# The last 32 dense tokens of a PEER layer: activations from gathered rows instead of a chunked product

## The chip, the cores and the metric

The kernel runs on one core of a Trainium2 chip. The metric is the device time of one launch in microseconds, as the median over several runs. A profile is one further execution, recorded by the hardware profiler. TensorE (PE) multiplies matrices and PEld is its weight load; VectorE (DVE), ScalarE (ACT) and GpSimd (POOL) work elementwise; SyncE (SP) only issues DMAs.

## What is computed

One decoder block over 512 tokens of width 1024. The change touches its second half, a PEER layer over 128 x 128 = 16384 experts of one neuron each:

```python
q = (xb @ w_pq).reshape(-1, PEER_HEADS, PEER_QDIM)          # 8 heads
s1 = einsum('thd,hkd->thk', q1, sub_k1); s2 = einsum('thd,hkd->thk', q2, sub_k2)
v1, i1 = top_k(s1, 16); v2, i2 = top_k(s2, 16)
cand = v1[..., :, None] + v2[..., None, :]
sc, ci = top_k(cand, 16)                                    # 16 experts per head, 128 per token
e = i1[ci // 16] * 128 + i2[ci % 16]
g = softmax(sc)
act = gelu(einsum('thkd,td->thk', peer_u[e], xb))
out = einsum('thk,thkd->td', g * act, peer_v[e])
```

Each token chooses 128 experts, takes the dot product of its row h2 with their rows of `peer_u`, applies GELU, weighs with g, and sums rows of `peer_v`. A LayerNorm follows.

## The kernel before

The 512 tokens are four tiles of 128 (P). The tiles 0 to 2 (DENSE = 3, SD = 384 tokens) are computed densely: all 16384 experts in NCH = 128 chunks of 128, first `act = gelu(U_chunk^T h2)` with the tokens as the 384 moving columns of a matmul, then the product of `act` with a dense weight matrix G (zero where a token has not chosen the expert), and last `acc += (act * G)^T V_chunk` into six PSUM banks of 128 x 512. Tile 3 is computed sparsely: 128 gathers of rows of `peer_u` and 128 of `peer_v`, each 128 rows of 4 KB, by indirect DMAs on GpSimd's queue, each multiplied on VectorE.

All products of float32 are made from three (`mm3`): each operand is split into a high part (ScalarE, `load_split2`, L450) and a low part, hi x hi + hi x lo + lo x hi. A chunk of U is 8 x 3 = 24 matmuls of 384 columns (L62 to L64), a chunk of V 3 x 2 x 3 = 18 of 512 columns (`V_products`, L797 to L801). The low part is made on GpSimd (L456) while `last["pool"]` is set, that is until the end of the top-k, and on VectorE (L458) from then on.

The stages of the second half, in the order of the program:

- 16 `query` and `scores` steps. After each, `pump(QPUMP)` runs background work of VectorE: `rows_h2` (h2 of tile 3 by rows, h2n), then one generator `topk_head(h)` per head.
- The main loop runs chunks of U as long as background work is left: the rest of the heads, `topk_last` (tile 3), `softmax`, then `spread`. Chunks until the end of the top-k are "spilled": `act` goes to DRAM (Ad) and comes back later.
- `spread` builds G: for 24 groups of TG = 16 tokens (q = 0 to 7 of each tile t) it makes one-hot matrices of the two index halves on VectorE (L631 to L635, f16), multiplies them on TensorE (L643, L644), scales on ScalarE into `stg` (L645) and writes G to DRAM (Gd). The first NRES = 21 chunks of this stage stay in SBUF ("resident", `U_resident`): their `act` and G are multiplied in place (L651, L653, L705). Further chunks, and VDLY = 3 more, are spilled.
- V of the 21 resident chunks, with GR = 1.8 steps of the gather of tile 3 per chunk.
- The rest in pairs: U and V of one chunk, with GUV = 2.9 gather steps per pair. G is loaded in runs of 8 chunks (1536 KB), and `wf = act * G` is made on VectorE (L778).
- V of the spilled chunks: `ar` brings four chunks of `act` back by one DMA (768 KB), G as before; the gather steps that are left are shared among all but the last six chunks. 260 steps stand for the whole gather.

Pacing is by credits. A generator yields the microseconds that its author declares for what it just issued, and `pump` spends a sum of them after each chunk of U:

```python
    def pump(us):
        credit[0] += us
        while credit[0] > 0 and bg:
            try:
                credit[0] -= next(bg[0])
            except StopIteration:
                bg.pop(0)
```

Before, the sum is 5.5 per query step (QPUMP), 1.1 + 1.2 = 2.3 per chunk until the end of the top-k (UPUMP), 5 in the spread (GPUMP). The order of instructions on an engine is in the end the framework's: it places an instruction by its own reckoning of when operands and buffers are ready, so that work can run ahead of its place in the program. So `rows_x1` (L495), issued in the stage of pairs, executes at 490 us, as soon as xhat is there, in the buffer `facc1`. `behind(a, b)` puts instruction a behind b in its queue. The row buffers of all gathers are four (tag "rows").

## Time and profile before

| | |
|---|---|
| median of 3 runs | 1719.38 us (1719.3 to 1720.42) |
| the profiled execution | 1727.59 us |
| its span, first to last instruction | 1725.9 us |
| mean granted TensorE clock | 0.991 of full |
| TensorE busy | 1668.0 us (97%) |
| VectorE busy | 1353.8 us (78%) |
| DMA | 409.92 MB, mean 238 GB/s |

The span is cut into stages by what runs: queries from about 485 us, chunks of U beside the top-k to 724, the spread to 885, the resident chunks' V to about 985, pairs to 1545, V of the spilled chunks to 1717, then the last LayerNorms. In the rows below a line of code stands as L and its number; PE and PEld are TensorE's matmuls and weight loads. A matmul's record lasts longer than the distance to the next, because matmuls overlap: the distance between starts is what counts.

### The profile page before, as it was taken

How to read it: one execution, taken by the hardware profiler on the slowest of the kernel's cores; microseconds unless marked ns; L12 is line 12 of the kernel's file. 1: busy time of each engine (PE TensorE's matmuls, PEld its weight loads, DVE VectorE, ACT ScalarE, POOL GpSimd, SP SyncE). 2: the span in 40 equal slices, each digit the busy share in tenths (PEclk: the TensorE clock that was granted, in tenths of full speed). 3: DMA queues.
4: the chain of work that ended last, by engine and by line, in shares of the span. 5: the costliest groups of instructions: out<-in, count | busy, mean ns of one | idle time of the engine just before them, and what ended most of it. 6: DMA issues, size and time to landing. Idle time of an engine off the chain costs nothing.

```text
span 1725.9 us, 23559 instructions
## 1 busy us (share of the span) xinstructions
PE 1668.0 (97%) x8658; PEld 1442.8 (84%) x8658; DVE 1353.8 (78%) x2509; ACT 685.9 (40%) x1095; POOL 481.5 (28%) x334
## 2 busy tenths in 40 slices
PE   6999999999999999899999999999999999989997
PEld 3765777788788999899998789999999999978886
DVE  6467786454589999999978888778787888878787
ACT  3467632233343333355543233333333333333333
POOL 2000000000043455400014444444454545531202
PEclk9999999999999999999999999999999999999999
DMA  7602257642252355556699999999899999899982
GB/s 269 201 1 74 98 196 245 219 146 86 77 189 78 103 173 172 191 206 224 211 321 365 363 325 340 320 338 351 312 337 324 326 345 324 311 351 316 305 282 86
DMA packets 162071, 409.92 MB, mean 238 GB/s; under 512 B 22337, under 2 KB 69473, under 8 KB 161698
## 3 DMA queue, kind: packets, MB, share of 16 engines
q1 hardware_dynamic: 112178, 245.35, 42.3%
q0 software_dynamic: 36960, 134.50, 21.6%
q10 hardware_dynamic: 12816, 28.55, 4.3%
q8 instruction: 68, 1.11, 0.3%
q14 instruction: 49, 0.40, 0.1%
HBM read 377.07 MB, written 31.01 MB: 236 GB/s over the span
## 4 chain that ended last, share of the span: by engine, by line
PE 55%; DVE 18%; DMA 5%; issue 4%; POOL 2%; ACT 0%; SPq 0%; DVEq 0%; POOLq 0%; ACTq 0%
PE acc L801 8%; PE acc L800 8%; PE acc L797 8%; PE psU L64 7%; PE psU L62 6%; PE psU L63 6%; DMA wa<-in_w_ada_dram 2%; POOL ru L667 2%; DMA ru<-in_peer_u_dram,idx 1%; DMA rawV<-in_peer_v_dram 1%; PE pso L63 1%; PE pso L64 1%; PE psga L64 1%; PE psga L62 1%; PE pspa L64 1%
## 5 line engine op out<-in xcount | busy, mean ns | idle before, releaser
L64 PE MATMUL psU<-h2Thi,loU 128*128 128x384 f32 x1008 | 340.6, 338 | 5.4 <-DVE loU L458 5.3
L62 PE MATMUL psU<-h2Thi,hiU 128*128 128x384 f32 x1008 | 340.8, 338 | 0.0
L63 PE MATMUL psU<-h2Tlo,hiU 128*128 128x384 f32 x1008 | 339.3, 337 | 0.0
L797 PE MATMUL acc<-hiV,wh 128*128 128x512 f32 x768 | 300.1, 391 | 4.5 <-ACT wh L782 4.5
L800 PE MATMUL acc<-loV,wh 128*128 128x512 f32 x768 | 301.5, 393 | 1.5 <-DVE loV L458 1.5
L801 PE MATMUL acc<-hiV,wl 128*128 128x512 f32 x768 | 301.1, 392 | 0.3 <-DVE wl L783 0.3
L667 POOL DMA_INDIRECT ru<-in_peer_u_dram,idx x128 | 159.0, 1242 | 360.6 <-DVE ru L671 341.2
L680 POOL DMA_INDIRECT rv<-in_peer_v_dram,idx x128 | 176.4, 1378 | 247.9 <-DVE facc L686 226.6
L458 DVE TENSOR_TENSOR loV<-rawV,hiV 128x1024 fp32r<-128x1024 f32 x128 | 156.4, 1222 | 101.2 <-ACT hiV L450 100.9
L450 ACT ACTIVATE hiV<-rawV 128x1024 fp32r<-128x1024 f32 x128 | 135.1, 1055 | 224.2 <-PE psU L63 184.1
L450 ACT ACTIVATE hiU<-rawU 128x1024 fp32r<-128x1024 f32 x126 | 134.0, 1063 | 194.5 <-PE psU L63 105.5
L64 PEld LDWEIGHTS psU<-h2Thi,loU 128*128 128x128 f32 x1008 | 190.4, 189 | 7.7 <-DVE loU L458 7.6
L63 PEld LDWEIGHTS psU<-h2Tlo,hiU 128*128 128x128 f32 x1008 | 190.6, 189 | 2.6
L62 PEld LDWEIGHTS psU<-h2Thi,hiU 128*128 128x128 f32 x1008 | 190.4, 189 | 2.6
L797 PEld LDWEIGHTS acc<-hiV,wh 128*128 128x128 f32 x768 | 144.9, 189 | 33.7 <-ACT wh L782 5.1
L671 DVE SCALAR_TENSOR_TENSOR ru<-ru,h2n 128x1024 f32<-128x1024 f32 x128 | 154.4, 1221 | 22.0 <-DMA ru<-in_peer_u_dram,idx 21.8
L800 PEld LDWEIGHTS acc<-loV,wh 128*128 128x128 f32 x768 | 144.8, 189 | 32.0 <-DVE loV L458 3.1
L801 PEld LDWEIGHTS acc<-hiV,wl 128*128 128x128 f32 x768 | 144.8, 189 | 31.1 <-DVE wl L783 0.7
L686 DVE SCALAR_TENSOR_TENSOR facc<-rv,wg,facc 128x1024 f32<-128x1024 f32 x126 | 159.4, 1278 | 11.7 <-DMA rv<-in_peer_v_dram,idx 11.7
L456 POOL TENSOR_TENSOR lopq<-rawpq,hipq 128x1024 fp32r<-128x1024 f32 x16 | 40.7, 2544 | 325.1 <-ACT hipq L450 325.1
L782 ACT ACTIVATE wh<-wf 128x384 fp32r<-128x384 f32 x107 | 56.2, 526 | 183.4 <-DVE wf L778 100.5
L458 DVE TENSOR_TENSOR loU<-rawU,hiU 128x1024 fp32r<-128x1024 f32 x95 | 115.7, 1218 | 1.4 <-ACT hiU L450 1.4
(628 smaller groups left out, 2942.4 us busy)
## 6 DMA issues: line engine op xcount, KB each, us to landing
rawU<-in_uT_dram SPq DMA_DIRECT2D x128, 512.0 KB
rawV<-in_peer_v_dram SPq DMA_DIRECT2D x128, 512.0 KB
wa<-in_w_ada_dram SPq DMA_DIRECT2D x48, 512.0 KB
G<-Gd SPq DMA_DIRECT2D x11, 1536.0 KB
Gd<-stg ACTq DMA_DIRECT2D x24, 592.0 KB
rawpq<-in_w_pq_dram SPq DMA_DIRECT2D x16, 512.0 KB
Ad<-act ACTq DMA_DIRECT2D x38, 192.0 KB
ar<-Ad SPq DMA_DIRECT2D x9, 768.0 KB
```

The source lines that it names most:

```text
L62: nc.tensor.matmul(ps, l.hi, r.hi, start=(i == 0), stop=False)
L63: nc.tensor.matmul(ps, l.hi, r.lo, start=False, stop=False)
L64: last = nc.tensor.matmul(ps, l.lo, r.hi, start=False, stop=(i == n - 1))
L450: h = nc.scalar.activation(hi, raw, AF.Copy)
L458: last["dve"] = nc.vector.tensor_sub(lo, raw, hi.bitcast(F32))
L667: d = nc.gpsimd.indirect_dma_start(out=rows, out_offset=None, in_=I["peer_u"], in_offset=bass.IndirectOffsetOnAxis(ap=idx[:, s:s + 1], axi ...
L671: paced(nc.vector.scalar_tensor_tensor(rows, rows, 1.0, h2n, op0=ALU.mult, op1=ALU.mult, accum_out=wg[:, s:s + 1]))
L680: nc.gpsimd.indirect_dma_start(out=rows, out_offset=None, in_=I["peer_v"], in_offset=bass.IndirectOffsetOnAxis(ap=idx[:, s:s + 1], axis=0))
L686: paced(nc.vector.scalar_tensor_tensor(fa, rows, wg[:, s:s + 1], fa, op0=ALU.mult, op1=ALU.add))
L797: m = nc.tensor.matmul(acc, l.hi, r.hi, start=st, stop=False)
L800: nc.tensor.matmul(acc, l.hi, r.lo, start=False, stop=False)
L801: nc.tensor.matmul(acc, l.lo, r.hi, start=False, stop=sp_)
```

## The change

The dense tokens become SU = 352 plus GX = 32. Chunks of U have 352 moving columns. For the last 32 tokens of tile 2 the activations of just the 128 chosen experts each are computed: `gather_x` copies the 32 x 128 indices into 128 partitions x 32 columns, gathers 32 times 128 rows of `peer_u`, multiplies each with h2x (the rows h2 of those 32 tokens, four times below each other) and sums, then applies GELU. The activations go into the weights before the one-hots are multiplied (`weights_x`, scaled by the largest value per token, and the scale put back on `stg`), and `act` of those columns is 1 everywhere. The steps of `gather_x` are spread over `topk_last` (one after every second step) and `spread` (one per group until none is left). The credits change: 2.0 per chunk for the heads (HPUMP), 2.8 from `topk_last` on (UPUMP, now without the 1.2), 4.0 in the spread (GPUMP).

```diff
@@ -26,16 +26,20 @@
 DENSE = 3
 SD = DENSE * P
 TG = 16
+GX = 32
+SU = SD - GX
+X0 = P - GX
 
 NTAIL = 4
 FPOOL = {0: 2, 1: 2, 2: 0, DENSE: 0}
-UPUMP = 1.1
+HPUMP = 2.0
+UPUMP = 2.8
 GUV = 2.9
 GU = 0
 NPRE = 2
 PLO = 1
 QPUMP = 5.5
-GPUMP = 5
+GPUMP = 4.0
 VDLY = 3
 NRES = 21
 GR = 1.8
@@ -389,10 +393,11 @@
 
         def early_U(i):
             w = load_split(I["uT"][i], f"U{i}")
-            ps = pmm.tile([P, D], F32, name=f"psU{i}", tag="ss", bufs=1)[:, 0:SD]
-            mm3(ps, [(w[:, k, :], h2T[:, k, 0:SD]) for k in range(NK)])
+            ps = pmm.tile([P, D], F32, name=f"psU{i}", tag="ss", bufs=1)[:, 0:SU]
+            mm3(ps, [(w[:, k, :], h2T[:, k, 0:SU]) for k in range(NK)])
             a = gp.tile([P, S], F32, name=f"act{i}", tag="mt", bufs=2)[:, 0:SD]
-            nc.scalar.activation(a, ps, AF.Gelu)
+            nc.scalar.activation(a[:, 0:SU], ps, AF.Gelu)
+            nc.gpsimd.memset(a[:, SU:SD], 1.0)
             nc.sync.dma_start(Ad[i], a)
 
         for hh in range(2):
@@ -432,6 +437,10 @@
     actp = ctx.enter_context(tc.tile_pool(name="actp", bufs=1, reuse_waits="tile"))
     gat = ctx.enter_context(tc.tile_pool(name="gat", bufs=1, reuse_waits="tile"))
     pu = ctx.enter_context(tc.tile_pool(name="pu", bufs=1, space=PS, reuse_waits="tile"))
+
+    acts = [actp.tile([P, SD], F32, name=f"act{i}") for i in range(4)]
+    for a in acts:
+        nc.gpsimd.memset(a[:, SU:SD], 1.0)
     last = {}
 
     def behind(ins, other):
@@ -465,6 +474,7 @@
 
 
     bg = []
+    last["upump"] = HPUMP
 
     credit = [0.0]
 
@@ -478,14 +488,45 @@
 
 
     h2n = gat.tile([P, D], F32, name="h2n", tag="facc0", bufs=1)
+    h2x = gat.tile([P, D], F32, name="h2x", tag="facc1", bufs=1)
 
     def rows_h2():
         g2r, b2r = (gat.tile([P, D], F32, name=nm, tag="rows", bufs=4) for nm in ("g2r", "b2r"))
         nc.sync.dma_start(g2r, rowsD[2].partition_broadcast(P))
         nc.sync.dma_start(b2r, rowsD[3].partition_broadcast(P))
-        nc.vector.tensor_mul(h2n, xhat[:, DENSE, :], g2r)
-        nc.vector.tensor_add(h2n, h2n, b2r)
-        yield 2.4
+        for t, h in ((DENSE - 1, h2x), (DENSE, h2n)):
+            nc.vector.tensor_mul(h, xhat[:, t, :], g2r)
+            nc.vector.tensor_add(h, h, b2r)
+            yield 2.4
+        for p in range(0, X0, GX):
+            nc.gpsimd.dma_start(h2x[p:p + GX, :], h2x[X0:P, :])
+
+
+    idxf = gat.tile([P, P], I32, name="idxf")
+    idxx = gat.tile([P, GX], I32, name="idxx")
+    wgx = gat.tile([P, GX], F32, name="wgx")
+    actx = gat.tile([P, P], F32, name="actx")
+
+    def gather_x():
+        nc.gpsimd.memset(actx, 1.0)
+        nc.vector.scalar_tensor_tensor(idxf, i1s[:, DENSE - 1, :], 128.0, i2s[:, DENSE - 1, :], op0=ALU.mult,
+                                       op1=ALU.add)
+        for j in range(P // GX):
+            d = nc.gpsimd.dma_start(idxx[j * GX:(j + 1) * GX, :], idxf[X0:P, j * GX:(j + 1) * GX])
+            behind(d, last["pool_lo"])
+        for s in range(GX):
+            rows = gat.tile([P, D], F32, name=f"rx{s}", tag="rows", bufs=4)
+            d = nc.gpsimd.indirect_dma_start(out=rows, out_offset=None, in_=I["peer_u"],
+                                             in_offset=bass.IndirectOffsetOnAxis(ap=idxx[:, s:s + 1], axis=0))
+            behind(d, last["pool_lo"])
+            m = nc.vector.scalar_tensor_tensor(rows, rows, 1.0, h2x, op0=ALU.mult, op1=ALU.mult,
+                                               accum_out=wgx[:, s:s + 1])
+            if "dve" in last:
+                behind(m, last["dve"])
+            yield 1.2
+        nc.scalar.activation(wgx, wgx, AF.Gelu)
+        for j in range(P // GX):
+            nc.gpsimd.dma_start(actx[X0:P, j * GX:(j + 1) * GX], wgx[j * GX:(j + 1) * GX, :])
 
     def rows_x1():
         for i, op in enumerate((ALU.mult, ALU.add)):
@@ -600,8 +641,12 @@
                     lambda a: a[:, 0:DENSE, 16 * h:16 * h + 16])
 
     def topk_last():
-        return topk("l_", 8, lambda half, j: sall[:, 2 * j + half, DENSE, :],
-                    lambda a: a[:, DENSE, :].rearrange("p (h k) -> p h k", h=8))
+        lanes = topk("l_", 8, lambda half, j: sall[:, 2 * j + half, DENSE, :],
+                     lambda a: a[:, DENSE, :].rearrange("p (h k) -> p h k", h=8))
+        for n, us in enumerate(lanes):
+            yield us
+            if n % 2 == 1:
+                yield step_x()
 
 
     def spread():
@@ -609,19 +654,53 @@
         gpool = gb.enter_context(tc.tile_pool(name="gpool", bufs=1, reuse_waits="tile"))
         pg = gb.enter_context(tc.tile_pool(name="pg", bufs=1, space=PS, reuse_waits="tile"))
         shp = [P, TG // 2, P, 2]
+
+        def weights_T(nm, pt):
+            gT = gpool.tile([P, 2, P], F16, name=f"gT{nm}", tag="gT", bufs=2)
+            nc.scalar.activation(gT[:, 0, :], pt, AF.Copy, scale=32768.0)
+            nc.vector.scalar_tensor_tensor(gT[:, 1, :], pt, 32768.0, gT[:, 0, :], op0=ALU.mult, op1=ALU.subtract)
+            return gT
+
+        def weights_x():
+
+            w = gpool.tile([P, P], F32, name="wx")
+            nc.vector.tensor_mul(w, gs[:, DENSE - 1, :], actx)
+            m = gpool.tile([P, 3], F32, name="mx2")
+            nc.vector.tensor_reduce(m[:, 0:1], w, AX.X, ALU.max)
+            nc.vector.tensor_reduce(m[:, 1:2], w, AX.X, ALU.min)
+            nc.vector.scalar_tensor_tensor(m[:, 0:1], m[:, 1:2], -1.0, m[:, 0:1], op0=ALU.mult, op1=ALU.max)
+            nc.vector.tensor_scalar(m[:, 0:1], m[:, 0:1], 1e-30, None, op0=ALU.max)
+            nc.vector.reciprocal(m[:, 2:3], m[:, 0:1])
+            nc.vector.tensor_scalar(w, w, m[:, 2:3], None, op0=ALU.mult)
+            mb = gpool.tile([P, P], F32, name="mb")
+            nc.vector.tensor_copy(mb, m[:, 0:1].to_broadcast([P, P]))
+            pt = pg.tile([P, 3, P], F32, name="ptx", tag="ptg", bufs=1)
+            nc.tensor.transpose(pt[:, 0, :], w, ident)
+            nc.tensor.matmul(pt[:, 1, :], mb, ident, start=True, stop=True)
+            sc = gpool.tile([P, P], F32, name="scx")
+            nc.scalar.copy(sc, pt[:, 1, :])
+            return weights_T("x", pt[:, 0, :]), sc
+
         for t in range(DENSE):
+            scx = None
             pt = pg.tile([P, 3, P], F32, name=f"ptg{t}", tag="ptg", bufs=1)
             for i, src in enumerate((i1s, i2s, gs)):
                 nc.tensor.transpose(pt[:, i, :], src[:, t, :], ident)
             iT = gpool.tile([P, 2, P], F16, name=f"iT{t}", tag="iT", bufs=2)
             nc.scalar.copy(iT, pt[:, 0:2, :])
-            gT = gpool.tile([P, 2, P], F16, name=f"gT{t}", tag="gT", bufs=2)
-            nc.scalar.activation(gT[:, 0, :], pt[:, 2, :], AF.Copy, scale=32768.0)
-            nc.vector.scalar_tensor_tensor(gT[:, 1, :], pt[:, 2, :], 32768.0, gT[:, 0, :], op0=ALU.mult,
-                                           op1=ALU.subtract)
+            gT = weights_T(t, pt[:, 2, :])
             yield 0.4
             for q in range(P // TG):
                 nm = f"{t}_{q}"
+                if t < DENSE - 1 or q < X0 // TG - 2:
+                    for _ in range(-(-left_x[0] // ((DENSE - 1 - t) * (P // TG) + X0 // TG - 2 - q))):
+                        yield step_x()
+                elif t == DENSE - 1 and q == X0 // TG - 2:
+                    step_x()
+                    nextx = weights_x()
+                    yield 1.8
+                if t == DENSE - 1 and q == X0 // TG:
+                    gT, scx = nextx
 
                 def tok(a, n=TG):
                     return (a[:, q * TG:q * TG + n].rearrange("p (a b) -> p a b", b=2).unsqueeze(2)
@@ -644,8 +723,12 @@
                         nc.tensor.matmul(ps[:, i, :], oh[0][sel], oh[2][sel], start=False, stop=True)
                     nc.scalar.activation(stg[:, :, 4 * b:4 * b + 4], ps.rearrange("p t i -> p i t"), AF.Copy,
                                          scale=1.0 / 32768.0)
-
-                c0, n = res["first"], len(res["ids"])
+                if scx is not None:
+                    nc.vector.tensor_mul(stg, stg, scx[:, q * TG:(q + 1) * TG].unsqueeze(1)
+                                         .to_broadcast([P, NCH, TG]))
+                    yield 2.3
+
+                c0, n = res["first"], len(res["ids"]) if t * P + q * TG < SU else 0
                 sl = slice(t * P + q * TG, t * P + (q + 1) * TG)
                 if n:
                     nc.vector.tensor_mul(res["tile"][:, 0:n, sl], res["tile"][:, 0:n, sl], stg[:, c0:c0 + n, :])
@@ -695,12 +778,12 @@
         w = load_split2(I["uT"][i], f"U{i}")
         ps = pu.tile([P, SD], F32, name=f"psU{i}", tag="mm", bufs=2)
         wv = Split(w.hi.rearrange("p (k c) -> p k c", k=NK), w.lo.rearrange("p (k c) -> p k c", k=NK))
-        last["U"] = mm3(ps, [(wv[:, k, :], h2T[:, k, 0:SD]) for k in range(NK)])
-        slot, n = res["tile"][:, len(res["ids"]), :], res["spread"]
-        if n < SD:
-            nc.scalar.activation(slot[:, n:], ps[:, n:], AF.Gelu)
+        last["U"] = mm3(ps[:, 0:SU], [(wv[:, k, :], h2T[:, k, 0:SU]) for k in range(NK)])
+        slot, n = res["tile"][:, len(res["ids"]), :], min(res["spread"], SU)
+        if n < SU:
+            nc.scalar.activation(slot[:, n:SU], ps[:, n:SU], AF.Gelu)
         if n:
-            a = actp.tile([P, SD], F32, name=f"act{i}", tag="act", bufs=4)
+            a = acts[i % 4]
             nc.scalar.activation(a[:, 0:n], ps[:, 0:n], AF.Gelu)
             nc.vector.tensor_mul(slot[:, 0:n], slot[:, 0:n], a[:, 0:n])
         res["ids"].append(i)
@@ -709,9 +792,9 @@
         w = load_split2(I["uT"][i], f"U{i}")
         ps = pu.tile([P, SD], F32, name=f"psU{i}", tag="mm", bufs=2)
         wv = Split(w.hi.rearrange("p (k c) -> p k c", k=NK), w.lo.rearrange("p (k c) -> p k c", k=NK))
-        last["U"] = mm3(ps, [(wv[:, k, :], h2T[:, k, 0:SD]) for k in range(NK)])
-        a = actp.tile([P, SD], F32, name=f"act{i}", tag="act", bufs=4)
-        nc.scalar.activation(a, ps, AF.Gelu)
+        last["U"] = mm3(ps[:, 0:SU], [(wv[:, k, :], h2T[:, k, 0:SU]) for k in range(NK)])
+        a = acts[i % 4]
+        nc.scalar.activation(a[:, 0:SU], ps[:, 0:SU], AF.Gelu)
         if not keep_act:
             nc.scalar.dma_start(Ad[i], a)
         return a
@@ -802,6 +885,13 @@
 
     last["pool"] = PLO > 0
     bg.append(rows_h2())
+    left_x = [GX]
+
+    def step_x():
+        left_x[0] -= left_x[0] > 0
+        return next(gx, 0.2)
+
+    gx = gather_x()
     qt = query(0, 0)
     for j in range(16):
         nxt = query((j + 1) // 2, (j + 1) % 2) if j < 15 else U_chunk(NPRE, False)
@@ -833,7 +923,12 @@
         return
         yield
 
-    bg += [topk_last(), softmax(), end_topk(), spread(), end_spread()]
+    def heads_done():
+        last["upump"] = UPUMP
+        return
+        yield
+
+    bg += [heads_done(), topk_last(), softmax(), end_topk(), spread(), end_spread()]
     gt = gather()
     n_g = 0
     spilled = list(range(NPRE + 1))
@@ -863,7 +958,7 @@
         else:
             U_chunk(i, False)
             spilled.append(i)
-            pump(GPUMP if res else UPUMP + 1.2 * bool(last.get("pool")))
+            pump(GPUMP if res else last["upump"])
         i += 1
     open_v()
     for _ in range(VDLY):
```

## Rows read from the trace of the kernel before

**Rows 1.** The head of the page: busy time, 40 slices, chain by engine.

```profile
PE 1668.0 (97%) x8658; PEld 1442.8 (84%) x8658; DVE 1353.8 (78%) x2509; ACT 685.9 (40%) x1095; POOL 481.5 (28%) x334
...
DMA  7602257642252355556699999999899999899982
GB/s 269 201 1 74 98 196 245 219 146 86 77 189 78 103 173 172 191 206 224 211 321 365 363 325 340 320 338 351 312 337 324 326 345 324 311 351 316 305 282 86
...
PE 55%; DVE 18%; DMA 5%; issue 4%; POOL 2%; ACT 0%; SPq 0%; DVEq 0%; POOLq 0%; ACTq 0%
```

**Rows 2.** Windows: length; busy PE, PEld, DVE, ACT, POOL (count); clock; DMA share; GB/s.

```profile
600.00:700.00 100.00, 100.00 (x579) 100.00 (x578) 99.97 (x437) 34.50 (x48) 59.28 (x25) 1.00 0.52 175
700.00:724.00 24.00, 19.63 (x114) 18.98 (x113) 23.45 (x54) 10.50 (x13) 9.65 (x6) 0.95 0.39 132
724.00:885.00 161.00, 157.83 (x1389) 151.89 (x1390) 154.30 (x188) 87.46 (x172) 2.61 (x2) 0.99 0.65 229
890.00:980.00 90.00, 88.52 (x394) 73.09 (x393) 75.49 (x115) 32.21 (x43) 44.60 (x36) 1.00 1.00 362
985.00:1545.00 560.00, 552.45 (x2783) 502.07 (x2781) 448.31 (x552) 202.26 (x269) 260.64 (x193) 1.00 0.94 332
1560.00:1660.00 100.00, 100.00 (x442) 82.80 (x442) 77.53 (x95) 36.97 (x50) 18.73 (x19) 1.00 0.92 309
```

**Rows 3.** Groups by line and shape: busy us, mean ns, idle before.

```profile
L671 DVE SCALAR_TENSOR_TENSOR ru<-ru,h2n 128x1024 f32<-128x1024 f32 x128 | 154.4, 1221 | 22.0 <-DMA ru<-in_peer_u_dram,idx 21.8
...
L456 POOL TENSOR_TENSOR loU<-rawU,hiU 128x1024 fp32r<-128x1024 f32 x31 | 76.5, 2468 | 61.4 <-ACT hiU L450 61.4
...
L778 DVE TENSOR_TENSOR wf<-act,G 128x384 f32<-128x384 f32 x67 | 36.9, 551 | 0.0
...
L634 DVE TENSOR_TENSOR oh<-oh,gT 128x2048 f16<-128x2048 f16 x24 | 29.2, 1217 | 0.0
...
L778 DVE TENSOR_TENSOR wf<-ar,G 128x384 f32<-128x384 f32 x40 | 22.0, 555 | 16.7 <-DMA ar<-Ad 15.8
```

**Rows 4.** Timeline of TensorE at the end of the top-k: start, us, instruction, idle before.

```profile
721.04 0.45 PE L64 MATMUL psU<-h2Thi,loU 128*128 128x384 f32 x1 [2.05 <-DVE loU L458]
...
723.98 0.45 PE L615 MATMUL ptg<-ident,gs 128*128 128x128 f32 x1 [2.32 <-DVE gs L595]
...
725.82 0.52 PE L62 MATMUL psU<-h2Thi,hiU 128*128 128x384 f32 x1
726.14 0.52 PE L63 MATMUL psU<-h2Tlo,hiU 128*128 128x384 f32 x1
```

**Rows 5.** Timeline of TensorE in U, five steps apart.

```profile
641.81 0.33 PE L62 MATMUL psU<-h2Thi,hiU 128*128 128x384 f32 x1
...
642.67 0.33 PE L64 MATMUL psU<-h2Thi,loU 128*128 128x384 f32 x1
```

**Rows 6.** Timeline of TensorE in V, five steps apart.

```profile
1599.73 0.39 PE L797 MATMUL acc<-hiV,wh 128*128 128x512 f32 x1
...
1600.86 0.39 PE L801 MATMUL acc<-hiV,wl 128*128 128x512 f32 x1
```

**Rows 7.** Timeline of TensorE in the scores: eight matmuls in one row.

```profile
511.08 1.05 PE L529 MATMUL pssc<-subk,qt 128*128 128x128 f32 x8
```

**Rows 8.** The chain that ended last, at three places: start, us, what.

```profile
498.46 4.82 DMA ln<-in_ln1r_dram
...
523.66 0.27 DVE ohlh__3687 L581
...
525.23 2.32 DVE ohlh__3687 L581
...
719.76 2.35 DVE loU L458 x2
```

**Rows 9.** Timeline of VectorE before the queries.

```profile
477.99 3.29 DVE L486 TENSOR_TENSOR h2n<-xhat,g2r 128x1024 f32<-128x1024 f32 x1
```

**Rows 10.** Windows, end of the resident stage; columns as in Rows 2.

```profile
940.00:990.00 50.00, 45.74 (x204) 37.36 (x202) 39.47 (x60) 15.32 (x19) 24.58 (x21) 1.00 0.97 362
```

## The prediction

> **What bounds the kernel now.** I read the head of the page first. TensorE is busy 97% of the span, VectorE 78%, and the DMA engines stand at nine tenths for most of the second half, at 305 to 365 GB/s [rows 1]. Half the chain that ended last is TensorE, but VectorE has 18% of it, so there are stages with another limit; the windows by stage show which [rows 2]. (1) Chunks of U beside the top-k (600 to 700): TensorE full, and VectorE full too (99.97 of 100 us). TensorE needs nothing from VectorE there, since the low halves are made on GpSimd (31 of 2.47 us) [rows 3]; the chunks of U are filler while VectorE works. (2) At 700 to 724 the filler is used up and TensorE stands 4.4 us; the timeline shows it waiting for the first low half and then for the softmax, and after it a granted clock of the lower level, 0.32 us between matmuls instead of 0.17 [rows 4]. (3) The spread (724 to 885): VectorE 154 of 161 us, TensorE 158. (4) The 21 resident chunks (890 to 980): DMA share 1.00 at 362 GB/s. (5) U and V in pairs (985 to 1545): DMA 0.94. (6) V of the spilled chunks (1560 to 1660): TensorE full, DMA 0.92 at 309 GB/s [rows 2]. So time in TensorE counts nearly everywhere, but VectorE stands right behind it until 885 and the DMA after it.
>
> **The change: what TensorE gets back.** Two points of the timeline give the price of a column: five steps of a 384-column matmul of U take 0.86 us, 172 ns each [rows 5], five of a 512-column matmul of V 1.13 us, 226 ns each [rows 6]. 128 columns cost 54 ns, 0.42 ns each, one column per cycle at 2.4 GHz. 32 columns fewer are 13.4 ns, 24 matmuls make 0.32 us a chunk, 128 chunks **-41 us**. The bound below is nothing, if the weight load (189 ns in the records, its engine 100 of 100 us busy at 600 to 700 [rows 2]) set the 172 ns. Against that: eight 128-column matmuls of the scores, each with its own 128x128 load, take 1.05 us with the tail of the last (0.27), 0.11 us apart [rows 7]. I take all 41. The Trainium skill ("TensorE: Matmul & The Clock Gate", "Back-to-back issue gap") says that in a stream of load and matmul pairs both set the spacing; read as a floor at 172 ns it would make the -41 a 0, and the 0.11 us speaks against such a floor. One transpose and one matmul are added, 0.5 us.
>
> **What is filled by how many chunks.** The loops pace the work by declared credits, so the number of chunks in each stage can be counted. A head of top-k declares 6x1.02 + 0.54 + 3x1.06 + 0.4 + 2x2.08 = 14.4, eight 115.2; the queries pay 16x5.5 = 88, of which rows_h2 takes 2.4 (now 4.8). There remain 29.6 (32.0). The last top-k is 36.2, softmax 1.9. Before: 67.7 at 2.3 a chunk, 30 chunks. After: 32.0 at 2.0, then 38.1 and 15 gather steps of 1.2 at 2.8: 37 chunks. Spread before: 24x5.1 + 1.2 = 123.6 at 5, 25 chunks; after: with 17 more steps, 1.8 and 2x2.3, 150.4 at 4, 38 chunks. Spilled in all: 3+30+4+3 = 40, now 3+37+17+3 = 60. Pairs of U and V: 67, now 47. The trace confirms 67 and 40 for before [rows 3]. Each pair runs 2.9 steps of the old gather and each resident chunk 1.8, of 260. So 27.9 steps were left for 34 spilled chunks (0.82 each); now 85.9 are left for 54 (1.59 each). That is the less visible half of this change.
>
> **Top-k.** VectorE gets 16 multiplies of gathered rows (1.22 and 0.08 us each [rows 3], about 1.2 in a row): 19 us; idxf 0.3; seven more GpSimd subtractions, during which an operation of VectorE can stand (2.32 us on the chain where its like takes 0.27 [rows 8]): 0 to 7. It loses something too: h2x takes the buffer facc1, in which rows_x1 ran ahead of everything at 490 to 512, with a wait of 4.8 us for its second load on the chain [rows 8]. Those 8 operations can come only when the last multiply of the spread has read h2x; with the wait that is 12 us. Net +8 to +14 on VectorE; TensorE gets seven more chunks of 24x0.159 = 3.8 us against 30x0.32 saved, +17. So the 6 us lost at 716 to 729 [rows 4] stay about as they are: **0**, between -5 (cover suffices) and +8. Of the added DMAs on GpSimd's queue the four copies of idxx wait for VectorE's idxf, and each gather for a buffer of rows that VectorE frees; queued behind them are the low halves of U, which have three buffers, so TensorE has two chunks of lead. That is the +8.
>
> **h2x.** Two more VectorE operations before the last low half of h2T. The like one, h2n, took 3.29 us [rows 9]. Between 0 (in a gap) and 6.6; **+3**. The three copies of h2x stand on GpSimd's queue before low halves that are due two queries (24x0.226 us each) later: 0.
>
> **Spread.** VectorE per step: four one-hots of 1.22 [rows 3], a row of such operations running 1.13 apart (two in 2.35 [rows 8]), and some 0.5 on the resident tile; per chunk a low half of 1.13 and up to 0.3. Before, 24x5.02 + 25x1.4 = 155, as long as its record (154). After, 120 + 38x1.13 + 6 + 17x1.2 + two multiplies of 2048 f32 (about 2.2 each, twice a low half) + 2 = 196. TensorE: the stage's 158 less 27 chunks of 4.13 leave 46 for the one-hot products; 38x3.82 + 46 = 191. VectorE led by some 6 us before (TensorE: 25x4.13 + 46 = 149) and does by 5 now: **+2**, between -2 and +10 (gathers that land late and hold the queue). The gather's activation and its copies come six steps before use. rows_x1 returns here or in the pairs, 8 operations and a load: **+1.5**, between 0 and 10.
>
> **Costed at nothing.** The memsets of the last 32 columns and the four fixed tiles for act, which rotate as four buffers did. The new gathers bring 16.8 MB and the 20 further chunks that go to Ad 3.9 MB, in stages where the DMA share is 0.39 to 0.65 [rows 2]; at 362 GB/s, without that cover, they would be 57 us.
>
> **Pairs.** A raw tile or a gather is 128x1024 f32, 0.524 MB; G 0.197 MB a chunk. 4.9x0.524 + 0.197 = 2.77 MB per 24x0.159 + 18x0.226 = 7.9 us, 350 GB/s, under the 362 that the resident stage moved [rows 2]: **+2**, 0 to 10.
>
> **Spilled V.** TensorE needs 18x0.226 = 4.07 us a chunk. The DMA must bring 0.524 + 0.197 of G + 0.197 of activations + 1.59x0.524 = 1.75 MB, 430 GB/s. No stretch of the trace moves that: 362 at share 1.00, and this stage's own 309 at 0.92, 336 at full share [rows 2]. At 362 a chunk takes 4.84 us, 0.77x54 = 41 us over; at 336 5.21, 62 over. What such an overload costs TensorE, the resident stage shows: 34 MB wanted in 86 us, 8 us too much at 362, and TensorE idle 4.3 us at 940 to 990 [rows 10]. Half was absorbed by what lay in the buffers; over a stage three times as long less is. I take three quarters of 41: **+31**, between 20 and 62. The Trainium skill ("DMA: Bandwidth & Descriptors", "Where 436 GB/s comes from") sets a limit of some 358 GB/s per core at the HBM and tells of 425 measured on one core with its neighbour idle. By 358 this term would be 45 at full conversion, by 425 nearly nothing; the share of 1.00 at 362 agrees with the first.
>
> **The sum.** -41 + 0.5 + 0 + 3 + 2 + 1.5 + 2 + 31 = -1 on the profiled execution's 1727.6 us. The median of the runs is 8.2 below that execution; taken over, 1718.4 us. A change under 0.2% (3.4 us) can hardly be told from none in this kernel.
>
> **Rivals.** (A) As computed, the DMA gives back most of the gain, and the terms fall within their middle bounds: 1700 to 1737. (B) The DMA keeps up in the spilled stage (the old gather lags and is absorbed, or the queues move over 420 GB/s): the 31 goes, 1687. For it: TensorE lost only 4.3 us in a stretch at share 1.00. Against: no slice above 365 [rows 1]. (C) The other side: the overload is paid at 336 GB/s in full, +62 in place of 31: 1749. It decides as soon as the overload is paid in full, 41 at 362 and more below that rate: then the stage alone takes back the gain. For it: the stage's own rate; against: more 4 KB rows in its mix. (D) GpSimd's queue stands behind the new gathers in the top-k, so low halves come late and each of 15 steps costs TensorE some 2 us: +30, 1748. Against: two chunks of lead. (E) The weight load sets the 172 ns and the columns save nothing: 1759.
>
> **Chances.** A 0.62, B 0.14, C 0.12, D 0.08, E 0.04. A lies around no change: 0.28 of it faster, 0.14 the same, 0.20 slower. Faster 0.28 + 0.14 = 0.42, same 0.14, slower 0.20 + 0.12 + 0.08 + 0.04 = 0.44. B's lower half, C's upper half and E, 0.17 in all, stay outside the range of 1687 to 1749.
>
> **What will show it.** Matmuls of U 159 ns apart (172 by E). 47 products of wf from act and 60 from ar, where 67 and 40 stand [rows 3]. The window of the spilled stage: share 1.00, near 360 GB/s, 4.6 to 4.9 us a chunk, VectorE's facc waiting for the rv gathers (A); 4.1 us and over 420 GB/s (B); 5.2 (C). At the end of the top-k, TensorE's wait of 4 to 9 us with the lower clock behind it; more, with GpSimd's ru-like gathers ahead of loU in the waits, is D. The prediction is wrong if the count of chunks per stage is not as worked out, or if the overload is not paid.

## The result, and the profile after

The changed kernel took 1749.97 us (median of 4 runs, 1745.02 to 1751.22) against 1719.9 for the kernel before on the same chip: a ratio of 1.0166, 95% interval 1.0142 to 1.0189: slower by 1.7%, clear of the noise. The profiled execution's span is 1743.3 us, 17.4 above that of before. The prediction's 1718.4 missed by 31 us, and the time lies just above its range. Head of the page of the changed kernel, lines as in [rows 1]:

```profile
PE 1638.0 (94%) x8661; PEld 1403.8 (81%) x8661; DVE 1393.4 (80%) x2572; ACT 682.8 (39%) x1097; POOL 581.1 (33%) x391
...
PEclk9999999999999998899999999999999999999998
DMA  7502267642252353687788999999999999999992
...
PE 45%; DVE 15%; issue 10%; DMA 9%; POOL 5%; ACT 0%; DVEq 0%; POOLq 0%; ACTq 0%
```

TensorE is busy 30 us less in a span that is 17 us longer: it waits more. Where, the windows of the changed kernel show (columns as in [rows 2]):

```profile
600.00:640.00 40.00, 40.00 (x251) 40.00 (x250) 40.00 (x147) 14.36 (x21) 26.23 (x11) 1.00 0.56 193
655.00:715.00 60.00, 27.97 (x149) 27.39 (x149) 57.55 (x248) 8.46 (x12) 23.65 (x16) 0.72 0.34 116
715.00:770.00 55.00, 55.00 (x343) 55.00 (x342) 30.95 (x22) 21.66 (x30) 50.51 (x27) 1.00 0.91 295
780.00:980.00 200.00, 198.69 (x1720) 194.40 (x1719) 197.01 (x241) 108.24 (x206) 24.91 (x19) 1.00 0.80 270
990.00:1065.00 75.00, 71.57 (x310) 57.41 (x308) 61.23 (x92) 25.51 (x34) 37.83 (x30) 1.00 0.98 353
1090.00:1440.00 350.00, 350.00 (x1852) 319.02 (x1851) 293.24 (x390) 131.81 (x178) 165.24 (x127) 1.00 0.97 346
1450.00:1700.00 250.00, 233.06 (x984) 182.45 (x984) 215.97 (x250) 83.23 (x109) 134.22 (x79) 1.00 1.02 366
```

The count tells more than the busy time. 149 matmuls of U at 0.160 us need 23.8 of the 60 us from 655 to 715: 36 us are lost in the top-k, where the kernel before loses 4.4 us at its end [rows 2]. 984 matmuls of V at 0.226 us need 222.4 of the 250 us from 1450 to 1700: 27.6 us are lost in the spilled V, where before lost nothing in 100 us [rows 2]. The spread and the pairs stand as predicted. GpSimd's timeline shows the first place:

```profile
650.24 2.40 POOL L465 TENSOR_TENSOR loU<-rawU,hiU 128x1024 fp32r<-128x1024 f32 x1 [1.47 <-ACT hiU L459]
664.53 1.99 POOL L515 DMA_DIRECT2D idxx<-idxf  x4 [11.90 <-DVE v0l__5400 L578]
666.54 2.35 POOL L465 TENSOR_TENSOR loU<-rawU,hiU 128x1024 fp32r<-128x1024 f32 x1
669.07 1.04 POOL L519 DMA_INDIRECT rx<-in_peer_u_dram,idxx  x1 [0.17 <-issue]
...
678.46 2.40 POOL L465 TENSOR_TENSOR loU<-rawU,hiU 128x1024 fp32r<-128x1024 f32 x1
706.62 1.70 POOL L519 DMA_INDIRECT rx<-in_peer_u_dram,idxx  x1 [25.75 <-DVE rx L522]
708.34 2.49 POOL L465 TENSOR_TENSOR loU<-rawU,hiU 128x1024 fp32r<-128x1024 f32 x1
```

The copies of idxx wait 11.90 us, until VectorE, still in the heads, has made idxf (at 663.96). The fifth gather waits 25.75 us for a row buffer, which VectorE frees with its first multiply of a gathered row; that comes at 705.12, behind the whole of the last tile's top-k, though the program issues a gather step after every second piece. Low halves stand behind both. TensorE's side is in the waits of 640 to 725 (us in total, times, longest):

```profile
PE psU L68 <- POOL loU L465: 32.0, 2, 24.2
POOL rx L519 <- DVE rx L522: 25.8, 1, 25.8
POOL idxx L515 <- DVE v0l__5400 L578: 11.9, 1, 11.9
```

The two waits for a low half are 32 of the 36 us; the other 4 are matmuls at the lower clock behind each wait (granted 0.72 over the window).

Waits of the spilled V in the changed kernel, 1450 to 1700:

```profile
ACT wh L865 <- DVE wf L861: 117.1, 30, 9.3
...
ACT hiV L459 <- DMA rawV<-in_peer_v_dram: 39.0, 15, 5.8
DVE facc L769 <- DMA rv<-in_peer_v_dram,idx: 30.1, 26, 2.8
...
PE acc L883 <- DVE loV L467: 12.2, 11, 2.2
```

VectorE stands in its own order behind gathers that have not landed, wf and loV come late, and ScalarE and TensorE after them.

### The profile page after: what moved, and what is told of

The parts are those of the page before. It is cut to its first block, busy times and chain, and to the rows that moved or that the text cites. A ratio compares the mean times of both kernels' runs of the same rounds, so it can differ in the third digit from the quotient of the medians.

```text
span 1743.3 us, 23737 instructions
## 1 busy us (share of the span) xinstructions
PE 1638.0 (94%) x8661; PEld 1403.8 (81%) x8661; DVE 1393.4 (80%) x2572; ACT 682.8 (39%) x1097; POOL 581.1 (33%) x391
## 4 chain that ended last, share of the span: by engine, by line
PE 45%; DVE 15%; issue 10%; DMA 9%; POOL 5%; ACT 0%; DVEq 0%; POOLq 0%; ACTq 0%
PE psU L68 7%; PE psU L66 7%; PE psU L67 7%; DMA rv<-in_peer_v_dram,idx 6%; PE acc L884 4%; PE acc L883 4%; PE acc L880 4%; POOL rv L763 2%; DMA wa<-in_w_ada_dram 2%; POOL ru L750 2%; PE psg L722 1%; PE pso L68 1%; PE psga L66 1%; PE pso L66 1%; PE pspa L66 1%
## 5 line engine op out<-in xcount | busy, mean ns | idle before, releaser
L68 PE MATMUL psU<-h2Thi,loU 128*128 128x352 f32 x1008 | 330.2, 328 | 36.1 <-POOL loU L465 32.0
L66 PE MATMUL psU<-h2Thi,hiU 128*128 128x352 f32 x1008 | 331.0, 328 | 0.0
L67 PE MATMUL psU<-h2Tlo,hiU 128*128 128x352 f32 x1008 | 328.4, 326 | 0.0
L763 POOL DMA_INDIRECT rv<-in_peer_v_dram,idx x128 | 205.2, 1603 | 168.2 <-DVE facc L769 137.6
L467 DVE TENSOR_TENSOR loU<-rawU,hiU 128x1024 fp32r<-128x1024 f32 x88 | 107.1, 1218 | 1.6 <-ACT hiU L459 1.5
L465 POOL TENSOR_TENSOR loU<-rawU,hiU 128x1024 fp32r<-128x1024 f32 x38 | 93.0, 2450 | 36.4 <-ACT hiU L459 36.1
## 6 DMA issues: line engine op xcount, KB each, us to landing
ar<-Ad SPq DMA_DIRECT2D x15, 768.0 KB, 11.4
```

Source lines behind the costliest of these rows:

```text
L66: nc.tensor.matmul(ps, l.hi, r.hi, start=(i == 0), stop=False)
L67: nc.tensor.matmul(ps, l.hi, r.lo, start=False, stop=False)
L68: last = nc.tensor.matmul(ps, l.lo, r.hi, start=False, stop=(i == n - 1))
L467: last["dve"] = nc.vector.tensor_sub(lo, raw, hi.bitcast(F32))
L763: nc.gpsimd.indirect_dma_start(out=rows, out_offset=None, in_=I["peer_v"], in_offset=bass.IndirectOffsetOnAxis(ap=idx[:, s:s + 1], axis=0))
```

## The experiments

Theory 1: the loss is GpSimd's in-order queue in the top-k. Theory 2: it is the transfers in the spilled V. Theory 3: VectorE is full wherever the change adds to it. Medians are in us; ratios are to the kernel before on the same chip, and 0.01 is 17 us. Diffs are against the changed kernel unless another is named.

**All gather steps in the spread.**

```
-            if n % 2 == 1:
-                yield step_x()
```

> All 32 gather steps are issued in the spread, none in the top-k of the last tile; nothing is left out. Theory 1 (GpSimd's in-order queue: index copies and gathers that wait for VectorE stand ahead of low halves of U): the 36 us that TensorE lost at 660 to 715 us are gone, GpSimd's low halves in the top-k stand 3.9 us apart, and the median is 1714 (1708 to 1720). Theory 2 (the transfers of the spilled V): the bytes are the same, two chunks fewer are spilled, so 1742 to 1750. Theory 3 (VectorE is what is full, in the top-k and in the spread): what leaves the top-k comes back in the spread, 1740 or more.

1732.72, 1.0068 (1.0046 to 1.0089): 17 us gained, half of what theory 1 said. The window of the top-k in that run:

```profile
655.00:715.00 60.00, 54.52 (x340) 54.21 (x338) 59.59 (x250) 22.89 (x32) 38.62 (x20) 0.97 0.56 186
```

340 matmuls instead of 149: with no gather step among the low halves the loss there is gone but for 7.5 us, and these are for a low half on VectorE. So theory 1 holds for the top-k, and half of what it gives is lost again later. VectorE is busy 226 of the 233 us from 709 to 942, which now hold all 32 steps, as theory 3 says.

**The order pinned.** Each multiply two steps after its gather, the next piece of top-k ordered behind it:

```
+            pend_x.append((rows, s))
+            if len(pend_x) > 2:
+                mult_x(*pend_x.pop(0))
...
-        nc.vector.max(vals[:, 0:8], src)
+        t16 = nc.vector.max(vals[:, 0:8], src)
+        if "mx" in last:
+            behind(t16, last["mx"])
```

> The gather steps stay in the top-k, but each multiply of a gathered row is issued two steps later than its gather and the next piece of top-k is ordered behind it on VectorE, so that a row buffer comes free every two pieces. Theory 1: GpSimd's wait of 25.8 us for a row buffer is gone, the wait of 11.9 us for the indices stays: 1728 (1722 to 1734). Theory 2: no change, 1745 to 1750. Theory 3: no change or slower, since VectorE now also waits for gathers.

1739.63, 1.0097 (1.0076 to 1.0118), 12 us gained. The long wait for a row buffer is gone (four waits, 11.5 us in all from 620 to 760), the 11.9 us for the indices stay. The gain is short of theory 1's 1722 to 1734.

**The late gathers left out.**

```
+            if s < 48:
+                rows = gat.tile([P, D], F32, name=f"rv{s}", tag="rows", bufs=4)
+                nc.gpsimd.indirect_dma_start(out=rows, out_offset=None, in_=I["peer_v"],
...
```

> Leaves out the gathers of rows of V from the 49th on (80 of 128, all of them in the stage of the spilled V) and multiplies the last gathered row again in their place, so that VectorE's instructions are the same; the output of the last tile's experts is not the reference's. Theory 2: TensorE's loss in the spilled V falls from about 33 us to about 8, so 1725 (1720 to 1731), with the DMA share there under 0.85. Rival: VectorE, busy 258 of the last 300 us, sets that stage, and nothing changes: 1745 to 1750.

1717.65, 0.9972 (0.9957 to 0.9987): 33 us. The window of that run, 1450 to 1700:

```profile
1450.00:1700.00 250.00, 248.61 (x1095) 204.98 (x1094) 242.90 (x293) 95.57 (x129) 7.30 (x3) 1.00 0.65 213
```

1095 matmuls instead of 984 with VectorE at 243 of 250 us: VectorE's work does not set this stage, the gathers do. Theory 2 holds for it, though this run does not tell the gathers' bytes from their buffers or their place on GpSimd's queue.

**The columns alone**, from the kernel before:

```
+SU = SD - GX
...
-            mm3(ps, [(w[:, k, :], h2T[:, k, 0:SD]) for k in range(NK)])
+            mm3(ps[:, 0:SU], [(w[:, k, :], h2T[:, k, 0:SU]) for k in range(NK)])
```

> The kernel before with 352 columns in each chunk of U and nothing else: no gathers for the 32 tokens, no second factor, the pacing of before; the activations of those 32 tokens are left at 1. If the columns are worth what the matmuls' spacing says: 3048 matmuls x 13.3 ns = 41 us less, 1679 (1675 to 1686). Rival: the shorter chunks reach the transfers and VectorE's work, which are no shorter, and half of the gain is lost in the top-k, the spread and the pairs: 1690 to 1700.

1711.25, 0.9933 (0.9908 to 0.9959). Only 12 of the 41 us arrive, less than either side expected. Its longest wait, 700 to 730:

```profile
PEld psU L66 <- DVE loU L465: 18.1, 1, 18.1
```

The first low half on VectorE stands behind the top-k. The same chunks take 0.32 us less each, so they cover 10 us less of the same VectorE work: theory 3. It does not cover the pairs, where TensorE stands 12 us in this run and next to nothing in the kernel before:

```profile
990.00:1525.00 535.00, 523.03 (x2739) 474.76 (x2738) 440.60 (x544) 195.68 (x265) 271.38 (x190) 0.99 0.95 339
```

```profile
990.00:1535.00 545.00, 544.65 (x2745) 495.69 (x2746) 440.11 (x542) 197.79 (x263) 256.84 (x191) 1.00 0.94 330
```

**The first gather step later**, at the tenth piece, on top of the pinned order:

```
-            if n % 2 == 1:
+            if n % 2 == 1 and n > 8:
```

> The run with the pinned order, and the first gather step comes at the tenth piece of the last tile's top-k and not at the second, so that the indices are there when GpSimd comes to their copies. Theory 1: GpSimd's wait of 11.9 us for the indices goes as well, 1728 (1723 to 1733) against 1739.6. Rival: VectorE's arrears set the end of the top-k, as in the run with the columns alone, and the wait only moves to the first low half on VectorE: 1736 to 1741.

1732.69, 1.0042 (1.0027 to 1.0058), 9 us better than the pinned order. But the idxx copies still waited 13.1 us: idxf is made in the same step and moved with them. So theory 1's number came without its cause, and what helped is not shown: four gathers fewer stand among the low halves, but TensorE waits as long for low halves on GpSimd as with the pinned order (10.9 and 11.4 us from 620 to 760).

**The credit of before in the spread**, on top of that run:

```
-GPUMP = 4.0
+GPUMP = 5
```

> The run above with the credit of before in the spread (GPUMP 5, not 4.0): by the credit arithmetic 51 chunks are spilled instead of 59, and 60 gathers of rows of V are left for their stage instead of 83. If only the transfers of the spilled V count: 23 gathers at 0.3 to 0.4 us each and the reads of eight chunks less, 10 to 16 us faster than the run above. If VectorE sets the spread (busy 224 of 230 us there in the changed kernel): eight chunks fewer stand under the same VectorE work, up to 31 us of TensorE's time, and it is 5 to 15 us slower than the run above.

1768.31, 1.0246 (1.0226 to 1.0266): 35 us slower than the run above. The window of 760 to 960, first of this run, then of the run above:

```profile
760.00:960.00 200.00, 181.28 (x1557) 171.13 (x1555) 192.51 (x248) 98.76 (x192) 38.66 (x27) 0.98 0.79 263
```

```profile
760.00:960.00 200.00, 195.21 (x1701) 191.32 (x1701) 194.68 (x243) 104.58 (x199) 33.52 (x24) 1.00 0.81 276
```

VectorE is as full in both; TensorE has less to do beside it, 144 matmuls or some 23 us. The spread lasts as long as VectorE's work, and 4.0 was needed to fill it. The other 12 us are lost behind the spread, and why is not shown.

**The columns alone, paced like the change**: in the run with the columns alone:

```
-UPUMP = 1.1
+HPUMP = 2.0
+UPUMP = 2.0
...
-GPUMP = 5
+GPUMP = 4.0
```

> The columns alone again (activations of the 32 tokens left at 1, no gathers), but with a pacing like that of the changed kernel (2.0 a chunk in the top-k, 4.0 in the spread), so that 52 chunks are spilled and not 41. If what took back 31 of the 41 us is VectorE's work per shorter chunk: the waits at the end of the top-k and in the spread go, 1688 (1682 to 1696). Rival: 11 more spilled chunks and 32 more gathers in the stage of the spilled V take as much as they give: 1706 to 1715, as in the run with the columns alone.

1705.11, 0.9882 (0.9862 to 0.9902): 20 of the 41 us. The waits at the end of the top-k and in the spread are gone, but with 63 gathers left for the spilled V that stage now loses some 30 of its 243 us (936 matmuls at 0.226). It lands between the two expectations.

**Sixteen tokens**, in the run with all steps in the spread:

```
-GX = 32
+GX = 16
...
-HPUMP = 2.0
-UPUMP = 2.8
+HPUMP = 2.15
+UPUMP = 2.5
...
-GPUMP = 4.0
+GPUMP = 4.5
```

> The change for 16 tokens instead of 32 (chunks of U of 368 columns, 16 gather steps, all in the spread, credits 2.15, 2.5 and 4.5); nothing is left out. The columns give 20 us instead of 41, 49 chunks are spilled instead of 58 and 54 gathers of rows of V are left for their stage instead of 80. By the transfers of the spilled V (73 MB in 267 us, 274 GB/s, no overload) some 28 us come back there: 1719 (1712 to 1726). Rival: the losses are those of GpSimd's and VectorE's queues, and half of the gain is lost with half of the gathers: 1727 to 1735.

1738.33, 1.0084 (1.0065 to 1.0104), no better than 32 tokens there. The bandwidth sum that promised 1719 misjudges this stage: at 1.26 gathers a chunk too TensorE loses some 30 of its 238 us (918 matmuls at 0.226).

**The indices apart**: their computation issued early, only their copies late, on top of the pinned order:

```
+        yield 0.1
         for j in range(P // GX):
             d = nc.gpsimd.dma_start(idxx[...
...
+            if n % 2 == 1 and (n == 1 or n > 8):
```

> The run with the late indices, but the indices themselves are computed at the first piece of the last tile's top-k and only their copies come at the tenth: in that run GpSimd still waited 13.1 us, since the computation had moved with the copies. Theory 1: that wait and TensorE's gap of 9.4 us behind it go, 1723 (1718 to 1728) against 1732.7. Rival: VectorE's arrears at the end of the top-k take its place, 1730 to 1735.

1730.63, 1.0045 (1.0029 to 1.0062): no better than the run before it. The indices were issued early but executed at 664.6, as soon as the heads had written what they are made of (664.4); GpSimd's wait for them fell from 13.1 to 5.9 us. Its windows at the end of the top-k:

```profile
640.00:715.00 75.00, 73.13 (x445) 72.84 (x444) 74.62 (x292) 26.81 (x38) 55.44 (x33) 0.98 0.72 236
715.00:770.00 55.00, 44.20 (x293) 42.79 (x292) 52.28 (x64) 20.35 (x32) 17.14 (x11) 0.84 0.62 205
```

TensorE runs nearly through to 715, and stands 10.8 us afterwards. Its waits from 715 to 770, and the gather that stands before the first of them:

```profile
PE psU L68 <- POOL loU L465: 3.9, 1, 3.9
PE ptg L701 <- DVE gs L649: 3.7, 1, 3.7
PE psU L68 <- DVE loU L467: 3.3, 1, 3.3
```

```profile
726.05 0.96 POOL L529 DMA_INDIRECT rx<-in_peer_u_dram,idxx  x1 [6.97 <-DVE rx L513]
```

Two of the three, 7.0 us, are VectorE's arrears (work of the top-k that it has not caught up with), as the rival says; the third is still GpSimd's queue. What the pinned order, the indices apart and the four gathers fewer took from that queue was together worth 1.0166 less 1.0045, 21 us.

**Gathers moved to the pairs**, in the run with the indices apart and in the paced columns:

```
-GUV = 2.9
+GUV = 3.4
```

> The run above, with 3.4 gathers a pair instead of 2.9: 24 gathers of rows of V leave the stage of the spilled V for the pairs, 59 in 53 chunks are left instead of 83. If that stage costs 0.3 us a gather (80 gathers gave 24 to 32 us): 7 to 9 us faster than the run above, 1715. Rival: the pairs' transfers, at a share of 0.97, have no room, and TensorE loses there what it gains later: no change against the run above, within 3 us.

> The columns alone with the changed pacing, and 3.4 gathers a pair instead of 2.9: 36 gathers in 46 chunks are left for the spilled V, 0.8 a chunk as in the kernel before, where that stage lost nothing. If the gathers a chunk decide and the pairs have room: the 38 us lost there fall to under 10, 1675 to 1682. Rival: the pairs lose it instead, 1700 to 1706 as before this edit.

1764.95, 1.0244 (1.0227 to 1.0261), and 1728.71, 1.0039 (1.0024 to 1.0055): 34 and 27 us slower, more than any expectation. In the paced columns the spilled V lost nothing any more from 1550 on, as in the kernel before; the pairs lost far more. The pairs of the first of the two runs, and of the run it was made from:

```profile
1100.00:1400.00 300.00, 281.93 (x1445) 253.00 (x1444) 248.04 (x325) 99.65 (x137) 165.54 (x116) 0.98 0.96 344
```

```profile
1100.00:1400.00 300.00, 300.00 (x1587) 273.47 (x1586) 247.48 (x330) 112.25 (x152) 146.01 (x107) 1.00 0.97 346
```

TensorE stands 18 us of the 300 and runs 142 matmuls fewer, some 27 us of its work, and the DMA moves no more than before. So something other than bandwidth was suspected: the four buffers for gathered rows.

**Five and three row buffers**, in the run with the indices apart, and the control. There is room for a fifth when act has two buffers.

```
-    acts = [actp.tile([P, SD], F32, name=f"act{i}") for i in range(4)]
+    acts = [actp.tile([P, SD], F32, name=f"act{i}") for i in range(2)]
...
-            rows = gat.tile([P, D], F32, name=f"rv{s}", tag="rows", bufs=4)
+            rows = gat.tile([P, D], F32, name=f"rv{s}", tag="rows", bufs=5)
```

> The run with the indices apart, with five buffers for gathered rows instead of four (and two act buffers instead of four, which make the room). If what the spilled V lacks is not bandwidth but row buffers (four buffers, each held from the gather's issue over some 8 us of landing to VectorE's turn, for 1.57 gathers each 5.46 us): the 30 us lost there fall by at least a third, 1720 or less against 1730.6. If it is bandwidth (a share of 1.0 at 345 to 370 GB/s): no change, 1728 to 1733.

> The control of the run with five row buffers: two act buffers instead of four and nothing else. By every theory no change against the run with the indices apart, 1728 to 1735; what it costs is to be taken off the comparison.

> The run with the indices apart, with three buffers for gathered rows instead of four. If the row buffers set the pace in the pairs and in the spilled V: three buffers carry at most 3 gathers in the 10 to 12 us that a buffer is held, fewer than the 1.57 in 5.46 us that are asked for, and it is 25 us or more slower, 1755 or more. If bandwidth does: the bytes are the same, 1728 to 1740.

Five: 1715.14, 0.9968 (0.9954 to 0.9981). Control: 1728.93, 1.0042 (1.0027 to 1.0057). Three: 1801.93, 1.0476 (1.0448 to 1.0504). The same bytes, and 74 us more or 13 less. With three, TensorE runs 1474 matmuls in the pairs from 1100 to 1400 instead of 1587, at a DMA share of 0.91. Waits of 1450 to 1700, first with four buffers, then with five:

```profile
ACT hiV L459 <- DMA rawV<-in_peer_v_dram: 32.3, 12, 6.5
DVE facc L782 <- DMA rv<-in_peer_v_dram,idx: 25.8, 19, 3.8
```

```profile
ACT hiV L459 <- DMA rawV<-in_peer_v_dram: 53.4, 24, 7.2
...
DVE facc L782 <- DMA rv<-in_peer_v_dram,idx: 11.2, 7, 2.8
```

With five, VectorE waits less for gathered rows (up to 1650, before either run leaves the stage, 11.2 us instead of 19.8), and ScalarE longer for the rows of V themselves. Windows of the same two runs, first four buffers, then five:

```profile
1000.00:1100.00 100.00, 95.28 (x452) 81.56 (x451) 84.33 (x125) 32.79 (x43) 49.31 (x40) 0.98 0.96 352
1400.00:1450.00 50.00, 45.45 (x218) 38.88 (x218) 42.32 (x48) 17.53 (x25) 30.09 (x17) 0.97 0.94 326
1450.00:1650.00 200.00, 189.90 (x793) 149.49 (x792) 170.82 (x195) 64.47 (x84) 103.90 (x66) 0.98 1.03 372
```

```profile
1000.00:1100.00 100.00, 98.63 (x482) 85.71 (x481) 87.93 (x131) 34.83 (x46) 52.70 (x42) 1.00 0.98 371
1400.00:1450.00 50.00, 50.00 (x242) 43.16 (x241) 41.27 (x48) 18.12 (x25) 30.91 (x17) 1.00 1.01 363
1450.00:1650.00 200.00, 188.87 (x787) 146.98 (x787) 174.27 (x200) 66.70 (x88) 119.93 (x68) 0.99 1.04 375
```

The gain lies at the borders: 30 matmuls more from 1000 to 1100, where the resident chunks end, and 24 more from 1400 to 1450, where the pairs end. Inside the spilled V both lose some 21 us of 200 (790 x 0.226 = 179) at the same 372 and 375 GB/s; there the fifth buffer changes nothing. That the DMA's rate is what limits there is argued, not shown; a sixth buffer was not tried.

**Five row buffers elsewhere**: with all steps in the spread, in the changed kernel as it stands, in the kernel before, and with 3.4 gathers a pair; the two edits are those shown above.

> The run with all 32 steps in the spread, with five row buffers and two act buffers; nothing is left out. If the row buffers are the limit: 1718 to 1722 against 1732.7, at or just under the kernel before. If bandwidth is: 1730 to 1735.

> The changed kernel itself with five row buffers and two act buffers, its gather steps where the change put them. If the buffers give 13 to 16 us behind the spread whatever stands ahead of it: 1733 (1728 to 1738) against 1750. The stall in the top-k is expected to stay: VectorE's first multiply of a gathered row is no earlier, and a fifth buffer lets one more gather by. Rival: the stall goes with it, 1715 to 1722.

> The kernel before with five row buffers and two act buffers. If its losses at the change from the spread to the resident chunks and from the pairs to the spilled V (7 us each) are also those of the four buffers: 1712 (1708 to 1717) against 1722. Rival: with 0.8 gathers a spilled chunk it lacks none, 1720 to 1725.

> The run with five row buffers, and 3.4 gathers a pair instead of 2.9. With four buffers that edit cost 35 us. If the buffers made it dear: it costs under 10 us or gains, 1705 to 1725. If the bandwidth of the pairs did: 1740 or more.

All steps in the spread: 1717.32, 0.9975 (0.9957 to 0.9993). The changed kernel: 1740.52, 1.0093 (1.0072 to 1.0115), 13 us better, its stall in the top-k still there (24.1 us). The kernel before: 1719.78, 0.9974 (0.9961 to 0.9987). More gathers in the pairs: 1735.61, 1.0055 (1.0035 to 1.0075), 15 us slower than with 2.9, where the same edit cost 34 with four buffers: about half of its price was the buffers. The rest may be the DMA, whose share in the pairs is then 0.99 at 362 GB/s; no run settles it.

The best version (order pinned, indices apart, five rows) beats both kernels, but the kernel before with five rows is as fast within the intervals. Mended, the change is worth nothing measurable.

## Why the prediction was wrong, point by point

- **What TensorE gets back, -41.** The spacing was right and the floor of rival E is refuted. Two rows of the changed kernel, five steps apart, are 0.80 us, 160 ns a step:

```profile
641.77 0.32 PE L66 MATMUL psU<-h2Thi,hiU 128*128 128x352 f32 x1
...
642.57 0.32 PE L68 MATMUL psU<-h2Thi,loU 128*128 128x352 f32 x1
```

  TensorE's own work fell by that much. Alone it gave 12 us, paced anew 20.
- **Chunk counts.** Right: 47 products from act and 60 from ar, GpSimd's low halves 38 instead of 31.

```profile
L465 POOL TENSOR_TENSOR loU<-rawU,hiU 128x1024 fp32r<-128x1024 f32 x38 | 93.0, 2450 | 36.4 <-ACT hiU L459 36.1
...
L861 DVE TENSOR_TENSOR wf<-ar,G 128x384 f32<-128x384 f32 x60 | 31.3, 550 | 0.7 <-DMA ar<-Ad 0.7
L861 DVE TENSOR_TENSOR wf<-act,G 128x384 f32<-128x384 f32 x47 | 25.9, 551 | 0.0
```

- **Top-k, 0. The step that failed.** TensorE loses 36 us there, 32 of them in two waits for low halves on GpSimd. Taking most of that queue's waits away gave 21 us; VectorE's arrears stand behind it. The sentence "each gather for a buffer of rows that VectorE frees; queued behind them are the low halves of U" named the mechanism, and two chunks of lead bounded it at +8. Rival D let the lead fail, at 15 steps of some 2 us. Its mechanism came true, and its +30 is the loss, but the size is luck: the loss is two waits, 7.8 and 24.2 us, and not 15 small ones. What both missed is where VectorE's multiply would stand. Four buffers carry four gathers; the fifth then waits for the rest of the top-k, 25.75 us at once, and two chunks of lead are 7.6 us.
- **h2x, +3; spread, +2; rows_x1, +1.5; pairs, +2.** None of the four shows. h2x executes from 489.3 us on, behind the last low half of h2T (484.6) and not ahead of it, and TensorE is busy 167.0 of the 170 us from 470 to 640, as before (166.8). It is busy 198.69 of 200 us in the spread and 350 of 350 in the pairs.
- **Spilled V, +31.** Right in sign and place: 27.6 us are lost in the window from 1450 to 1700, and the run without the late gathers gave 33. That it came so near is partly luck, since the three quarters were chosen. The reason was half right. 366 GB/s at a share of 1.02 fits "no stretch moves 430"; but 13 us of the changed kernel's time go with one more row buffer and not a byte less (in the run with the indices apart they come back at the borders of the stages). The argument that bandwidth alone sets it would have missed the 74 us of three buffers.
- **The sum.** -1 was predicted, the spans differ by +17.4. The top-k is 30 of that (36, less the 6 that the kernel before loses there); against it stand the four small costs that stayed away (8.5) and some 3 us of the spilled V (27.6 for 31). The other 13 of the 31 are the step from the profiled execution to the median, taken over as -8.2; for the changed kernel it is +5.

## What to carry to other kernels

When a gather goes onto a queue that also makes operands, ask where the consumer that frees its buffer stands in its own engine's order, in the built order and not in the program's: the price of a full ring is the whole distance to it, not a step. Count buffers against issue-to-release time before blaming bandwidth: one more and one fewer buffer with the same bytes is a cheap test. Shortening the filler beside an engine that is already full gives back only what that engine's slack allows, so price a saving stage by stage.

## What was not expected of the hardware

A multiply of a gathered row takes 1.22 us alone, and stood for 7.62 while GpSimd ran three low halves back to back. VectorE's row of the changed kernel, then GpSimd's:

```profile
744.83 7.62 DVE L522 SCALAR_TENSOR_TENSOR rx<-rx,h2x 128x1024 f32<-128x1024 f32 x1 [1.42 <-DMA rx<-in_peer_u_dram,idxx]
```

```profile
744.25 7.11 POOL L465 TENSOR_TENSOR loU<-rawU,hiU 128x1024 fp32r<-128x1024 f32 x3
```

Over the 32 steps the mean is 1815 ns, and 1225 with all steps in the spread, where GpSimd makes no low halves: 19 us of VectorE that the prediction priced at 0 to 7. By the Trainium skill ("SBUF — State Buffer", "SBUF: two separate sides") an operation of VectorE with two SBUF inputs and one of GpSimd that reads SBUF share a port pair: whichever starts first has it for its whole instruction, and the other stands. The two rows agree: the multiply ends 1.09 us after the third low half and got no turn between the three. The prediction had a smaller case of it, 2.32 us [rows 8]; the 0.27 set beside it there is another, larger operation of that line, and its true like (128x96) takes 0.20.

The prediction took a share of 1.00 for a full DMA at 362 GB/s [rows 2]. From 940 to 990 the kernel before moved 362 at 0.97 [rows 10]; with five row buffers, in the same window:

```profile
940.00:990.00 50.00, 49.28 (x229) 41.89 (x227) 44.79 (x68) 16.55 (x22) 32.07 (x24) 1.00 1.02 404
```

404 GB/s at 1.02: a share of 1.0 is no ceiling, and 362 was none. The Trainium skill ("Perfetto Trace Analysis", "Roofline") puts what one core can draw alone at some 120% of 358 GB/s; this window is at 113%.
